# A hybrid attention and state-space layer on one core: another order of the seven block products, the second token half's index queries before the first's, the first conv group in pairs, and a third pair of buffers for split weights

## The chip, the core and the metric

The kernel runs on one core of a Trainium2 chip. The metric is the time of one execution on the device in microseconds (us); less is better. Each time is the median of several runs on one chip, and one more execution was taken by the hardware profiler. In the profile, PE is the matrix engine, PEld its loading of the stationary operand, DVE the vector engine, ACT the scalar (activation) engine, POOL the general engine, and SP the engine whose queue issues the DMAs.

## The reference, cut to what matters

One layer over 1024 tokens of width 2048. All input projections are one product with `w_in`; its columns are then split by use.

```
u = einsum('bsd,de->bse', h, w_in)
q, k, v, z_attn, q_idx, k_idx, w_idx, z_ssd, xbc, dt_raw = split(u)
# indexer: 16 heads of 64, keys in chunks of 64; the top 256 keys of each query
logits = relu(einsum('bqhd,bsd->bqhs', rope(q_idx), rope(k_idx)))
score  = einsum('bqhs,bqh->bqs', logits, w_idx * c), causal by chunk
o_attn = attention(q, k, v over the selected keys) * silu(z_attn)
# mixer: causal depthwise conv (4 taps) and silu on xbc, then a scan over chunks
o_ssd  = gated_rmsnorm(ssd(silu(conv(xbc)), dt), silu(z_ssd))
h = layer_norm(alpha * h + concat(o_attn, o_ssd) @ w_out)
```

Everything is float32. The conv needs the last three tokens of the first half as its start in the second half.

## The kernel before, in words

**Precision.** A float32 operand is split on chip into a rounded high part and a remainder (`hi` on ACT, `lo = x - hi` on DVE, or on POOL where the planner's method `two`, line 473, picks it). A product of two such operands is three matmuls, hi·hi, hi·lo and lo·hi (lines 1181 to 1183 for the input projection). Weights are split in `w_split` (line 916) from a raw tile `wr` into `wh` and `wl`, 128x1024 each, that is a block of 1024 rows of the depth by 128 columns. Tokens are split in `t_xst` (line 766) into `xh` and `xl`, 128x512 each.

**Input projection.** Tokens stand in two halves (h = 0 the first 512, h = 1 the rest), the depth in two halves (u = 0 and 1). A *set* is one token half by one depth half, or a sum of such blocks: eight pairs `xh`, `xl`. There are 16 slots of each, so two sets are on chip at a time, and a set's slots come free one by one in the last product that reads it. A *product* is one set by one weight block into one PSUM tile `pj`: 8 pieces of the depth by 3 matmuls, 24 matmuls. A *plain* column tile takes two products for each token half, so eight in all for two tiles and both halves. A *pair* of column tiles is done with a Winograd scheme in seven products (`product`, line 665), over sets that are blocks of x or sums of them: `M2`, `M3`, `S1`, `S4` are made once by `t_xform` (line 783) and kept in device memory. A pair runs in four phases, with two products in each of the first three and one in the last. Between phases partial results (`P1`, `U2`, `U3`) go to device memory and back, and where a product needs a sum of weight blocks, `t_wacc` (line 880) makes it on DVE from raw tiles.

**Order of the work.** `PLAN` (line 56) lists the stages; a stage in round brackets is plain, one in square brackets is a group of pairs, in which phase by phase all pairs are passed. `misc` holds the indexer's keys and head weights and the mixer's dt; `qi` are the eight tiles of index queries (two heads each); `xbc` of group g is four tiles (two of x, one of B, one of C). For `qi` of the first half only the last 256 tokens are computed, as the first 256 have at most 256 keys to choose from: those products are 24 matmuls of 128x256 (`s0`, line 607).

```
PLAN = [
    (0, FIRST + [("xbc", (0, 2)), ("xbc", (0, 3))], 2),
    (1, [("misc", 0)] + QI + [("xbc", (0, j)) for j in range(4)], 3),
    [(("k", 0), ("k", 1)), (("v", 0), ("v", 1))] + [(("q", n), ("q", n + 4)) for n in range(4)],
    (0, QI, 3),
    [(("xbc", (1, j)), ("xbc", (3, j))) for j in range(4)] + ... # 14 pairs in all
]
```

So there are five stages: first half `misc` and conv group 0; second half `misc`, `qi` and conv group 0; the *first group*, six pairs of k, v and q; first half `qi`; the *second group*, 14 pairs. Then comes the output projection, seven products of 8 blocks (`PRODUCTS`, line 68), whose sums of `w_out` are made in the background by `t_wsum` (line 814) during the input projection.

**Index scores and selection.** When a `qi` tile is done, `t_qi` (line 1455) ropes and splits it and then adds, for each of its heads, each block of 128 queries and each half of the keys, two matmuls into a PSUM tile `a` and a task `t_score` (line 1496): a relu on ACT in place, and a multiply-add on DVE into the running score tile. The second half has 8 tiles x 2 heads x 4 blocks x 2 key halves = 128 such scores, the first half 32. When all are in, `t_topk` (line 1520) finds the threshold by 32 sweeps of ACT over the scores, each followed by three tiny DVE operations.

**What sets the order.** The program is written by a planner in Python: `Flow` (line 354) with a model of the engines `Sim` (line 132). It walks the products in their order on PE and between them emits background tasks when its model says that their inputs, buffers and engine are ready. On the chip each engine runs its own queue in the order written, with semaphores between. SP's queue holds nearly all DMAs, in order, so that a waiting DMA holds up those behind it.

Of the kernel before, what the change touches and what calls it, by code (L numbers as in the profile page):

```python
# [15 lines left out]
D = 2048  # L16
S = 1024
HALF = 512
P = 128
# [10 lines left out]
NU = 28  # L30
# [11 lines left out]
def tile_order():  # L42
# [10 lines left out]
FIRST = [("misc", 0), ("xbc", (0, 0)), ("xbc", (0, 1))]  # L53
KVQ = [("k", 0), ("k", 1), ("v", 0), ("v", 1)] + [("q", n) for n in range(8)]
# [77 lines left out]
class Sim:  # L132
# [154 lines left out]
    def dma(self, eng, out, in_, kw):  # L287
# [9 lines left out]
        self.clk["D"] = x + max(out.size(), in_.size()) * 4 * (1 / 400 + 0.6 / row)  # L297
# [259 lines left out]
class Piece:  # L557


    def __init__(self, kind, h=0, t=0, u=0, **kw):  # L560
        self.kind, self.h, self.t, self.u = kind, h, t, u
        self.load, self.keep, self.s0, self.n, self.last = (), (), 0, None, False
        self.open = self.close = True
        self.done = self.after = None
        self.hold = self.base = False
        self.op = ALU.add
        self.__dict__.update(kw)


class Layer:  # L570
    def __init__(self, ctx, tc, a):
# [7 lines left out]
        for tag, n in (("xh", 16), ("xl", 16), ("xr", 2), ("wr", 5), ("wh", 2), ("wl", 2), ("u", NU), ("s4", N4), ("cv", 2), ("sm", 6)):  # L579
            fl.add_tag(tag, pool("p_" + tag, bufs=1), n)  # L580
# [10 lines left out]
    def units(self):  # L591
# [3 lines left out]
        self.sets = []  # L595

# [15 lines left out]
        for pairs in PLAN:  # L612
# [10 lines left out]
            a11 = len(self.sets)  # L623
            base = a11 + 1
            self.sets += [("x", 1, 0), ("f", "M2"), ("f", "M3"), ("x", 0, 1), ("f", "S1"), ("f", "S4"), ("x", 1, 1)]
            n = [(a11, base), (base + 1, base + 2), (base + 3, base + 4)]
# [3 lines left out]
            for ph in range(3):  # L630
                for couple in couples:
                    for f in range(2):
                        for c in couple:
                            i = put(self.product(gi, c, pairs[c], ph, f, n[ph][f]))
                            if ph and not (ph == 1 and f == 1):
                                self.hooks.setdefault(max(i - 1, 0), []).append(lambda gi=gi, c=c, ph=ph, f=f: self.pre_ld(gi, c, ph, f))
            for c in range(len(pairs)):
                i = put(self.product(gi, c, pairs[c], 3, 0, base + 5))
                self.hooks.setdefault(i - 1, []).append(lambda gi=gi, c=c: self.pre_ld(gi, c, 3, 0))
# [25 lines left out]
    def product(self, gi, c, pair, ph, f, n):  # L665
# [7 lines left out]
        p = Piece("T", load=load, keep=keep, n=n, open=f == 0, close=True, skip=f == 1, key=(gi, c, ph),  # L673
                  hold=ph < 2 and f == 0, base=ph < 2 and f == 1)
        if f:
            p.after = self.ev_after(gi, c, ph)
        out = lambda h, k: (pair[k][0], h, pair[k][1])

        def done(ps):
            at = fl.t + 100  # L680
            if ph == 0:
                fl.add(self.t_save(gi, c, f, ps), 0, f"save{gi}{c}{f}", at)
            elif ph == 1 and f == 0:
                fl.add(self.t_u3(gi, c, ps), 0, f"u3{gi}{c}", at)
            else:
                kind, h, j = out(0, 0) if ph == 1 else out(0, 1) if ph == 2 and f == 0 else out(1, 1) if ph == 2 else out(1, 0)
                fl.add(self.t_comb(gi, c, ph, f, kind, h, j, ps), 0, f"{kind}{j}h{h}", at)
# [12 lines left out]
    def t_save(self, gi, c, f, ps):  # L700
# [4 lines left out]
        fl.act(x, ps)  # L705
        if f:
            fl.free(ps)
        else:
            fl.signal(self.ev_after(gi, c, 0))
        yield Need("")  # L710
        name = ("P1", "U2")[f]
# [4 lines left out]
    def t_u3(self, gi, c, ps):  # L716
        fl = self.fl
        yield Need("V", u=1, ev=(self.ev_ld[gi, c, 1, 0],))
        x = fl.new("u", [P, HALF])
        fl.tt("V", x, ps, self.ld[gi, c, 1, 0], ALU.add)  # L720
        fl.signal(self.ev_after(gi, c, 1))
        yield Need("")
        fl.dma(self.p_scr("U3", gi, c), x)
        fl.free(x)
        fl.signal(self.ev_save["U3", gi, c])

    def pre_ld(self, gi, c, ph, f):
        name = "P1" if ph == 3 else "U3" if (ph, f) == (2, 0) else "U2"
# [10 lines left out]
    def t_comb(self, gi, c, ph, f, kind, h, j, ps):  # L739

        fl = self.fl
        key = (gi, c, ph, 0 if ph == 1 else f)
        yield Need("V", ev=(self.ev_ld[key],), **({"cv": 1} if kind == "xbc" else {}))
        x = self.ld.pop(key)
        op = ALU.subtract if ph == 2 else ALU.add
        u = fl.new("cv", [P, 3 + HALF]) if kind == "xbc" else None
        fl.tt("V", x if u is None else u[:, 3:3 + HALF], ps, x, op)
        if (ph, f) == (2, 0):
# [3 lines left out]
        if u is None:  # L752
            yield from getattr(self, "s_" + kind)(h, j, x)
        else:
            yield from self.s_xbc(h, j, x, u)
# [27 lines left out]
    def t_xform(self, kp):  # L783
# [4 lines left out]
        for tag, h, u in (("s4", 0, 0), ("s4", 0, 1), ("xr", 1, 0)):  # L788
# [16 lines left out]
        fl.dma(d, self.a["xt"][1, 4 + kp])  # L805
# [8 lines left out]
    def t_wsum(self, half):  # L814
# [11 lines left out]
        for d in range(2):  # L826
            for j in range(4):
                yield Need("D", u=2, keep=6)
                x, y = load("B22", d, j), load("B12", d, j)
                yield Need("V")  # L830
                fl.two(x, x, y, ALU.subtract)
                yield Need("D", us=1)
                save("T3", d, j, x)
                fl.free(x)
# [3 lines left out]
                fl.free(z)  # L838
# [1449 lines left out]
```

## Time and profile before

| | us |
|---|---|
| median of 3 runs | 1727.53 |
| lowest and highest run | 1725.99, 1731.79 |
| the profiled execution's own time | 1725.14 |
| its span, first to last instruction | 1723.4 |

The profiled execution thus has 1.7 us around its span, and its time lies 2.4 us under the median. How to read the profile: a row of groups gives an instruction's line, engine, operation, what it writes and reads, shapes, how many, then its busy time and mean duration, then the idle time of the engine before it and what ended that. Nearly every instruction carries line 313, a helper, so tiles tell them apart: `pj` is PSUM for products, `a` PSUM for scores and transposes, `wr` a raw weight tile, `u` and `s4` general buffers (`s` in some rows). A table of windows gives busy time and count of each engine in a stretch of the span, then PEclk, the granted clock of PE as a share of full speed. Matmuls overlap: one of 128x512 is reported with some 390 ns, but the next may start 227 ns later, so a full PE shows as busy throughout, and work is counted by starts, not by busy time.

### The profile page before, as it was taken

What the parts mean: (1) busy time and instruction counts of PE and PEld (TensorE: products, weight loads), DVE (VectorE), ACT (ScalarE), POOL (GpSimd) and SP (SyncE); (2) the same over time, 40 slices, a digit from 0 to 9 for tenths busy, and PEclk for the clock granted to TensorE, in tenths of its full rate; (3) what the DMA queues carried; (4) which work ended last, traced back from release to release, by engine and by line L of the source; (5) the groups of instructions that cost most, each with busy time, mean ns of one, the idle gap of its engine ahead of it and who ended that gap; (6) DMA issues with size and microseconds to landing.
All of it is one profiled execution on the core that took longest, in us unless ns stands there. A gap on an engine that the chain in (4) does not pass through costs nothing. (4 is left out here: it accounts for less than half of the span.)

```text
span 1723.4 us, 24378 instructions
## 1 busy us (share of the span) xinstructions
PE 1638.7 (95%) x8044; PEld 1351.2 (78%) x8044; DVE 1353.0 (79%) x2444; ACT 1019.6 (59%) x1799; POOL 173.5 (10%) x201
## 2 busy tenths in 40 slices
PE   9999999998887989999999999989999999999997
PEld 7877788876666978778888788877888877888875
DVE  5779999787567898789996788845777677659998
ACT  5745575678666856987555478456867544532320
POOL 0000010000000000000222111222121110000110
PEclk9999999999899999999999999999999999999998
DMA  9576578988787678989666875658778999877654
GB/s 320 202 253 230 198 258 290 324 310 307 246 294 259 222 266 271 315 299 318 227 220 219 312 236 188 220 186 251 241 230 280 313 314 342 298 278 268 218 193 147
DMA packets 210215, 446.50 MB, mean 259 GB/s; under 512 B 21928, under 2 KB 61992, under 8 KB 210088
## 3 DMA queue, kind: packets, MB, share of 16 engines
q1 hardware_dynamic: 209656, 444.55, 75.9%
q8 instruction: 63, 1.03, 0.2%
q14 instruction: 64, 0.52, 0.1%
q10 hardware_dynamic: 432, 0.39, 0.1%
HBM read 338.56 MB, written 106.30 MB: 258 GB/s over the span
## 5 line engine op out<-in xcount | busy, mean ns | idle before, releaser
L313 PE MATMUL pj<-xh,wh 128*128 128x512 f32 (+1 forms) x1192 | 470.0, 394 | 25.9 <-ACT wh L313 18.0
L313 PE MATMUL pj<-xh,wl 128*128 128x512 f32 (+1 forms) x1192 | 460.1, 386 | 9.3 <-DVE wl L313 9.1
L313 PE MATMUL pj<-xl,wh 128*128 128x512 f32 (+1 forms) x1192 | 458.8, 385 | 0.1
L313 DVE TENSOR_TENSOR wl<-wr,wh 128x1024 fp32r<-128x1024 f32 (+1 forms) x179 | 213.9, 1197 | 113.2 <-ACT wh L313 112.6
L313 PEld LDWEIGHTS pj<-xh,wh 128*128 128x128 f32 x1192 | 227.1, 191 | 70.7 <-ACT wh L313 20.6
L313 PEld LDWEIGHTS pj<-xh,wl 128*128 128x128 f32 x1192 | 226.5, 190 | 58.8 <-DVE wl L313 14.4
L313 PEld LDWEIGHTS pj<-xl,wh 128*128 128x128 f32 x1192 | 227.3, 191 | 41.2 <-DVE xl L313 1.8
L313 ACT ACTIVATE wh<-wr 128x1024 fp32r<-128x1024 f32 (+1 forms) x185 | 190.6, 1033 | 106.7 <-PE pj L313 67.2
L313 PE MATMUL pj<-xh,s 128*128 128x512 f32 (+1 forms) x688 | 222.1, 385 | 1.8 <-DVE u L313 1.6
L313 PE MATMUL a<-u,u 128*128 128x512 f32 (+3 forms) x746 | 171.7, 351 | 16.4 <-DVE u L313 7.0
L313 PEld LDWEIGHTS a<-u,u 128*128 128x128 f32 x746 | 123.3, 189 | 50.1 <-DVE s L313 10.6
L313 PEld LDWEIGHTS pj<-xh,s 128*128 128x128 f32 x688 | 127.7, 188 | 27.3 <-ACT xh L313 2.3
L313 DVE TENSOR_TENSOR u<-u,u 128x512 f32<-128x512 f32 (+7 forms) x212 | 130.2, 627 | 16.1 <-DMA u<-wo 4.5
L313 ACT ACTIVATE u<-s,sm 128x768 bf16<-128x768 f32 (+7 forms) x132 | 129.6, 982 | 21.3 <-DVE sm L313 19.5
L313 DVE TENSOR_TENSOR wr<-wr,wr 128x1024 f32<-128x1024 f32 (+1 forms) x98 | 121.6, 1243 | 20.5 <-DMA wr<-wt 19.4
L313 ACT ACTIVATE u<-a 128x512 fp32r<-128x512 f32 (+4 forms) x115 | 53.4, 479 | 138.0 <-DVE u L313 66.5
L313 PE MATMUL pj<-xl,s 128*128 128x512 f32 (+1 forms) x344 | 130.8, 380 | 0.8 <-DVE xl L313 0.8
L313 ACT ACTIVATE u<-u 128x512 f32<-128x512 f32 (+4 forms) x165 | 91.9, 566 | 61.5 <-DVE u L313 57.3
L313 ACT ACTIVATE a<-a 128x512 f32<-128x512 f32 (+3 forms) x160 | 76.1, 504 | 70.3 <-PE a L313 69.2
L313 DVE TENSOR_TENSOR s<-wr,s 128x1024 fp32r<-128x1024 f32 (+2 forms) x59 | 70.8, 1200 | 30.7 <-ACT s L313 30.5
L313 DVE TENSOR_TENSOR u<-pj,u 128x512 f32<-128x512 f32 (+2 forms) x94 | 62.4, 664 | 36.7 <-PE pj L313 31.0
L313 PE MATMUL pj<-wh,xh 128*128 128x512 f32 x218 | 87.8, 403 | 1.2 <-DVE u L313 1.2
(253 smaller groups left out, 2678.9 us busy)
## 6 DMA issues: line engine op xcount, KB each, us to landing
wr<-wt SPq DMA_DIRECT2D x228, 512.0 KB, 5.3
u<-u SPq DMA_DIRECT2D x100, 256.0 KB, 5.7
u<-wo SPq DMA_DIRECT2D x79, 256.0 KB, 5.1
wr<-ts SPq DMA_DIRECT2D x32, 512.0 KB, 5.7
ts<-u SPq DMA_DIRECT2D x63, 256.0 KB, 4.3
xr<-xt SPq DMA_DIRECT2D x28, 512.0 KB, 4.9
s<-xt SPq DMA_DIRECT2D x28, 512.0 KB, 6.6
u<-mx SPq DMA_DIRECT2D x49, 256.0 KB, 6.3
```

What stands on the lines that cost most here:

```text
L313: f(*args, **kw)
```

## The change

The core of the diff; what is left out are the plumbing of the partial results' names, and the loops' unchanged lines.

```diff
-NU = 28
+NU = 29
...
-FIRST = [("misc", 0), ("xbc", (0, 0)), ("xbc", (0, 1))]
+FIRST = [("misc", 0), ("qi", 0), ("qi", 1)]
 PLAN = [
-    (0, FIRST + [("xbc", (0, 2)), ("xbc", (0, 3))], 2),
-    (1, [("misc", 0)] + QI + [("xbc", (0, j)) for j in range(4)], 3),
-    [(("k", 0), ("k", 1)), (("v", 0), ("v", 1))] + [(("q", n), ("q", n + 4)) for n in range(4)],
-    (0, QI, 3),
+    (1, FIRST + QI[2:], 3),
+    (0, [("misc", 0)] + QI, 3),
+    [(("k", 0), ("k", 1)), (("v", 0), ("v", 1))] + [(("q", n), ("q", n + 4)) for n in range(4)]
+    + [(("xbc", (0, 2 * j)), ("xbc", (0, 2 * j + 1))) for j in range(2)],
...
-        self.clk["D"] = x + max(out.size(), in_.size()) * 4 * (1 / 400 + 0.6 / row)
+        self.clk["D"] = x + max(out.size(), in_.size()) * 4 * (1 / 360 + 0.6 / row)
...
-        for tag, n in (("xh", 16), ("xl", 16), ("xr", 2), ("wr", 5), ("wh", 2), ("wl", 2), ("u", NU), ("s4", N4), ("cv", 2), ("sm", 6)):
+        for tag, n in (("xh", 16), ("xl", 16), ("xr", 2), ("wr", 6), ("wh", 3), ("wl", 3), ("u", NU), ("s4", N4), ("cv", 2), ("sm", 6)):
...
-            self.sets += [("x", 1, 0), ("f", "M2"), ("f", "M3"), ("x", 0, 1), ("f", "S1"), ("f", "S4"), ("x", 1, 1)]
+            if self.sets[-2:] != [("x", 0, 0), ("x", 0, 1)]:
+                self.sets += [("x", 0, 0), ("x", 0, 1)]
+            base = len(self.sets) - 2
+            self.sets += [("f", "M2"), ("f", "M3"), ("f", "S1"), ("f", "S4"), ("x", 1, 1)]
...
-        t3 = ("s", "T3", gi, c)
-        load, keep = [[((b11,), ()), ((b22, b12), (t3,))], [((t3,), ()), ((b11, b21), ())],
-                      [((b12, b11), ()), ((b22,), ())], [((b21,), ())]][ph][f]
+        t2 = ("s", "T2", gi, c)
+        load = [[(b11,), (b21,)], [(b22, b12, b11), ()], [(t2, b22), ()], [(t2, b21)]][ph][f]
...
-        for tag, h, u in (("s4", 0, 0), ("s4", 0, 1), ("xr", 1, 0)):
+        for tag, h, u in (("s4", 1, 0), ("s4", 1, 1), ("xr", 0, 0)):
...
-        for hh, st in ((0, a1), (1, a2)):
-            head = 2 * j + hh
...
-                for kh in range(h + 1):
...
+        for kh in range(h, -1, -1):
+            for hh, st in ((0, a1), (1, a2)):
+                head = 2 * j + hh
...
+        if first:
+            yield Need("A", cv=1, ev=(self.ev_carry[4 * j[0] + j[1]],))
+            u = fl.new("cv", [P, 3 + HALF])
+            fl.act(u[:, 3:3 + HALF], x)
...
-    nc = bacc.Bacc("TRN2", target_bir_lowering=False, num_devices=1)
+    nc = bacc.Bacc("TRN2", target_bir_lowering=False, num_devices=1, dynamic_dma_scratch_size=1024)
```

In words. **Stages.** There are four input stages in place of five: second half `misc` and `qi`; first half `misc` and `qi`; the first group, now eight pairs with conv group 0 as two of them; the second group as before, 14 pairs. Conv group 0 has no plain products any more. **Products of a pair.** Still seven in four phases, but the first phase is first token half by `b11` and by `b21`, the next `M2` and `M3`, then `S1` and `S4`, then the second half's second depth block. The weight block of a phase's second product is what is left of the first's sum (the new table `mate`): one list of loads in the second and the third phase serves two products. A pair loads 9 raw tiles in place of 10, and DVE makes 4 sums of them in place of 5. **Sets.** The first half's two sets are those that the stage ahead of the first group has used, and they stay. **Scores and conv.** In `t_qi` the scores of a tile go by key half, the queries' own half first. In `t_comb` a conv tile's second-half result can come ahead of its first-half result, and then waits in a buffer for the carried tokens. **Buffers.** A sixth raw tile, a third `wh` and `wl`, one more `u`; the scratch for the DMA rings of the general engine is set to 1024 bytes. **Output weights.** `t_wsum` keeps a tile that it used to load twice.

The planner writes the queues anew. Two places.

The first is PE's queue in the `qi` stage of the first token half. Before, these rows stand near the stage's start (`pj` is the product, `xh` and `xl` the tokens, `wh` and `wl` the weights):

```order
L313 MATMUL pj_5256<-xh_4845,wh_5123 128x256
L313 MATMUL pj_5256<-xl_4846,wh_5123 128x256
L313 MATMUL pj_5256<-xh_4845,wl_5124 128x256
L313 MATMUL pj_5256<-xh_4849,wh_5123 128x256
L313 MATMUL pj_5256<-xl_4850,wh_5123 128x256
L313 MATMUL pj_5256<-xh_4849,wl_5124 128x256
```

Now, in the same stage (`a` is a score's PSUM tile, `u_1716` to `u_1718` the first half's keys, `u_687` and `u_797` queries of the second half):

```order
L312 MATMUL pj_2076<-xl_1369,wh_1936 128x256
L312 MATMUL pj_2076<-xh_1368,wl_1937 128x256
L312 MATMUL a_2121<-u_1716,u_687 128x512
L312 MATMUL a_2121<-u_1718,u_687 128x512
L312 MATMUL a_2124<-u_1716,u_797 128x512
L312 MATMUL a_2124<-u_1717,u_797 128x512
L312 MATMUL a_2127<-u_1716,u_687 128x512
L312 MATMUL a_2127<-u_1718,u_687 128x512
L312 MATMUL pj_2076<-xh_1416,wh_1993 128x256
```

The narrow products stood by themselves; now the second half's scores against the first half's keys stand between them.

The second is SP's queue where the first group goes to its second phase: the sets (`xfM` is `M3` before and `M2` now, `xt` a block of x) and weights (`wt`). Before, from the middle of the loads of the first of the two sets:

```order
L313 DMA s_605_3316<-xfM_107 128x1024
L313 DMA s_610_3326<-xfM_108 128x1024
L313 DMA xr_3336<-xt 128x1024
L313 DMA p_0_5_3344<-u_3328 128x512
L313 DMA xr_3346<-xt 128x1024
L313 DMA wr_3359<-wt 128x1024
L313 DMA wr_3360<-wt 128x1024
L313 DMA s_620_3369<-xt 128x1024
L313 DMA s_625_3396<-xt 128x1024
```

Now, from the start of the loads of the first set:

```order
L312 DMA xr_3483<-xfM_109 128x1024
L312 DMA xr_3485<-xfM_110 128x1024
L312 DMA s_609_3487<-xfM_111 128x1024
L312 DMA s_610_3489<-xfM_112 128x1024
L312 DMA q_0_293<-u_3466 4x32x512
L312 DMA wr_3527<-wt 128x1024
L312 DMA wr_3528<-wt 128x1024
L312 DMA wr_3529<-wt 128x1024
L312 DMA t_0_0_3540<-wr_3425 128x1024
```

The four loads of a set stand in one run, ahead of the phase's weight loads, where they were spread among other transfers and those of the second set; three raw tiles are loaded at once for the two products of a pair, and their sum of two is kept (`t_0_0`).

More of the change, by code (lines that the diff above doesn't have):

```diff
@@ L705, in t_save, with t_u @@
         fl.act(x, ps)
+        fl.signal(self.ev_after(gi, c, 0))
+        yield Need("")
+        fl.dma(self.p_scr("P1", gi, c), x)
+        fl.free(x)
+        fl.signal(self.ev_save["P1", gi, c])
+    def t_u(self, gi, c, f, ps):
+        fl = self.fl
+        name = ("U2", "U3")[f]
+        yield Need("V", ev=(self.ev_ld[gi, c, 1, 0],), **({} if f else {"u": 1}))
+        y = self.ld[gi, c, 1, 0]
+        x = y if f else fl.new("u", [P, HALF])
+        fl.tt("V", x, ps, y, ALU.add)
         if f:
@@ L714, in t_save @@
         fl.signal(self.ev_save[name, gi, c])
[L716 to L725, printed above, removed]
     def pre_ld(self, gi, c, ph, f):
-        name = "P1" if ph == 3 else "U3" if (ph, f) == (2, 0) else "U2"
+        name = "P1" if ph == 1 else "U2" if f else "U3"
         e = self.ev_ld[gi, c, ph, f] = Event()
@@ L741, in t_comb @@
         fl = self.fl
-        key = (gi, c, ph, 0 if ph == 1 else f)
-        yield Need("V", ev=(self.ev_ld[key],), **({"cv": 1} if kind == "xbc" else {}))
+        key = (gi, c, ph, f)
+        first = (ph, f) == (2, 0)
+        cv = kind == "xbc" and not first
+        yield Need("V", ev=(self.ev_ld[key],), **({"cv": 1} if cv else {}))
         x = self.ld.pop(key)
[L745 to L748, printed above, removed]
+        u = fl.new("cv", [P, 3 + HALF]) if cv else None
+        fl.tt("V", u[:, 3:3 + HALF] if cv else x, ps, x, ALU.subtract if ph == 2 else ALU.add)
+        if first:
             fl.signal(self.ev_after(gi, c, 2))
@@ L751, in t_comb @@
             fl.free(ps)
[L752 removed]
+        if kind != "xbc":
             yield from getattr(self, "s_" + kind)(h, j, x)
[L754 to L755 removed]
+            return
+        if first:
+            yield Need("A", cv=1, ev=(self.ev_carry[4 * j[0] + j[1]],))
+            u = fl.new("cv", [P, 3 + HALF])
+            fl.act(u[:, 3:3 + HALF], x)
+        yield from self.s_xbc(h, j, x, u)
     def form_tasks(self):
@@ L863, in w_load @@
         fl = self.fl
+        if not p.load:
+            return
         if len(p.load) > 1:
@@ L956, in need_w @@
                 self.nld += 1
-            fl.drain(until=lambda: k not in self.wacc and self.w_room(), why="w")
+            fl.drain(until=lambda: k in self.wraw and self.w_room(), why="w")
             self.w_split(k)
@@ L1513, in t_score @@
                 fl.free(*self.kk[1])
-            else:
+            if sum(self.nlog) == 160:
                 fl.free(*self.kk[0])
@@ L1666, in s_v, with t_zs @@
         fl.signal(self.ev_kv[h, g, "v"])
+    def t_zs(self, h, gj, ps):
+        fl = self.fl
+        yield Need("A", u=1)
+        x = fl.new("u", [P, HALF])
+        yield from self.s_zs(h, gj, x, ps)
     def s_z(self, h, n, x):
```

156 lines of the change are left out of this document (73 added, 83 removed).

## The prediction

> **What bounds the kernel now.** The page's busy list comes first.
>
> ```profile
> PE 1638.7 (95%) x8044; PEld 1351.2 (78%) x8044; DVE 1353.0 (79%) x2444; ACT 1019.6 (59%) x1799; POOL 173.5 (10%) x201
> ```
>
> PE is the bound, so the time is PE's work plus what PE loses, and the work has to be counted. The timeline of PE gives the price of a matmul from start to start where nothing waits: eleven starts of the 128x512 form, then six of the 128x256 form.
>
> ```profile
> 701.05 0.39 PE L313 MATMUL pj<-xh,wl 128*128 128x512 f32 x1
> ...
> 703.32 0.39 PE L313 MATMUL pj<-xh,wh 128*128 128x512 f32 x1
> ```
>
> ```profile
> 548.77 0.28 PE L313 MATMUL pj<-xh,wh 128*128 128x256 f32 x1
> ...
> 549.37 0.28 PE L313 MATMUL pj<-xh,wl 128*128 128x256 f32 x1
> ```
>
> That is (703.32 - 701.05) / 10 = 0.227 us and (549.37 - 548.77) / 5 = 0.12 us. A product of 24 is 5.45 us, a narrow one 2.9. Next come windows cut at the stages: phases two to four of the first group, the narrow stage (first half `qi`), the second group in two pieces.
>
> ```profile
> core 0: us, PE busy (x) PEld busy (x) DVE busy (x) ACT busy (x) POOL busy (x), PEclk, DMA share, GB/s
> 340.00:548.00 208.00, 183.40 (x795) 144.96 (x795) 149.70 (x316) 145.63 (x267) 4.88 (x3) 0.96 0.84 290
> 548.00:615.00 67.00, 52.77 (x409) 50.81 (x409) 57.45 (x116) 52.46 (x87) 2.81 (x2) 0.92 0.67 237
> 680.00:1100.00 420.00, 415.44 (x2106) 347.03 (x2105) 343.94 (x679) 287.93 (x521) 63.24 (x64) 1.00 0.77 259
> 1100.00:1200.00 100.00, 91.24 (x472) 75.06 (x471) 57.53 (x117) 51.80 (x85) 19.82 (x19) 0.98 0.69 219
> ```
>
> The second group's first 420 us leave PE idle for 4.6 us. The first group's 208 leave 24.6, and the clock there is 0.96, another 0.04 x 208 = 8.3: 33 together. The count of work says the same. PE's groups by shape in 340:548:
>
> ```profile
> L313 PE MATMUL pj<-xh,wh 128*128 128x512 f32 x190 | 78.6, 413 | 15.1 <-ACT wh L313 7.3 <-ACT xh L313 6.8 <-DVE sm L313 0.8
> L313 PE MATMUL pj<-xh,wl 128*128 128x512 f32 x191 | 77.5, 406 | 5.0 <-DVE wl L313 5.0
> L313 PE MATMUL pj<-xl,wh 128*128 128x512 f32 x190 | 76.6, 403 | 0.1
> L313 PE MATMUL pj<-xh,s 128*128 128x512 f32 x96 | 31.4, 394 | 1.6 <-DVE u L313 1.6
> L313 PE MATMUL pj<-xl,s 128*128 128x512 f32 x48 | 18.7, 390 | 0.0
> ```
>
> These 715 take 162.3 us, the other 80 are at most 256 wide in this answer, so at most 9.6: 172 of 208, a loss of 36. The narrow stage in the same way:
>
> ```profile
> L313 PE MATMUL pj<-xh,wh 128*128 128x256 f32 x91 | 26.9, 296 | 9.1 <-ACT wh L313 9.1
> L313 PE MATMUL pj<-xh,wl 128*128 128x256 f32 x91 | 26.9, 295 | 2.0 <-DVE wl L313 2.0
> L313 PE MATMUL pj<-xl,wh 128*128 128x256 f32 x91 | 26.5, 292 | 0.0
> L313 PE MATMUL pj<-xh,s 128*128 128x256 f32 x64 | 12.9, 282 | 0.0
> L313 PE MATMUL pj<-xl,s 128*128 128x256 f32 x32 | 9.0, 282 | 0.0
> ```
>
> 369 x 0.12 = 44.3, the other 40 at most 0.227 each and mostly narrower, an estimated 6: some 51 of 67, a loss of 16. Each narrow product asks for a weight block of 512 KB every 2.9 us, 180 GB/s for weights alone, and its split by ACT and DVE besides.
>
> The waits of PE tell what the first group's idle time is made of (total, times, longest):
>
> ```profile
> PE pj L313 <- ACT wh L313: 7.3, 2, 5.8
> PE pj L313 <- ACT xh L313: 6.8, 2, 3.5
> PE pj L313 <- DVE wl L313: 5.0, 4, 3.6
> ```
>
> They are few and long: a split weight block or set that comes late when the sets are switched, with a DMA share of 0.84 and much of ACT's time taken.
>
> **The change, part by part.** All sums are made against the profiled execution, 1725.14 us; it lies 2.4 below the median of 1727.53, and I add that at the end.
>
> *Conv group 0 in pairs.* Four tiles took 16 plain products; two pairs take 14. 2 x 24 = 48 matmuls of 128x512 go, 48 x 0.227 = **-10.9 us**. In the order of the two programs nothing else differs on PE in number (5920 against 5872 of this shape). This is on the bound itself; the bounds are 0 and -10.9, since time saved on PE can turn into waiting.
>
> *The first group's waits.* Phases two to four make five switches of sets in both versions, but over 8 pairs x 5 = 40 products in place of 30, so 8 products (44 us) stand between switches in place of 6 (33 us). At each switch SP has four set loads of 512 KB in front of the weights (the second place of the order shown above): 2.1 MB at the window's 290 GB/s is 7.2 us. A split pair in reserve is one product, 5.45 us; the third `wh` and `wl` give a second, 10.9 us of cover against 7.2, and the sixth raw tile one more loaded behind it. The waits for `wh` and `wl`, 7.3 + 5.0 = 12.3, should go, and with the long idle stretches gone the clock's 8.3. The waits for `xh`, 6.8, are not covered by a weight buffer; with 8 products in place of 6 I take off a third, 2.3. Together **-23**, of a loss of 36; bounds 0 (what is late is the set, and the weights only stood behind it) and -36. Next late is then `xh`.
>
> *The narrow stage.* First half `qi` now stands right behind the second half's `qi`, and second-half scores lie between its narrow products, as the order shows. Scores need PE and no weights: between PE's rows 440 and 1342 of the new order, the latter at the end of the narrow products, I count 264 product matmuls of 128x512, 384 of 128x256, 176 score matmuls of 128x512 and 85 smaller, 158 us of PE work for about 27 weight blocks, one per 5.8 us in place of 2.9. The weight wait goes: **-16**. Bounds 0 and -16; if half stays, +8 on the sum.
>
> *What the scores ask of DVE there.* The nearest stretch of before is that of second-half scores, 126.5 to 222.8.
>
> ```profile
> 126.50:222.80 96.30, 94.31 (x424) 75.61 (x423) 91.86 (x140) 58.22 (x108) 4.22 (x3) 1.00 0.57 202
> ```
>
> DVE is busy 95% of it. PE's groups there, by shape:
>
> ```profile
> L313 PE MATMUL pj<-xh,wh 128*128 128x512 f32 x97 | 38.3, 395 | 0.0
> L313 PE MATMUL pj<-xh,wl 128*128 128x512 f32 x96 | 37.5, 390 | 0.0
> L313 PE MATMUL pj<-xl,wh 128*128 128x512 f32 x96 | 37.4, 390 | 0.0
> L313 PE MATMUL a<-u,u 128*128 128x512 f32 x83 | 24.5, 402 | 1.7 <-DVE s L313 1.6
> ```
>
> 372 x 0.227 = 84.4, and 52 smaller at some 0.13: 91 of 96.3, a loss of 5. For the new stretch I price DVE's 292 rows with the groups of the whole trace:
>
> ```profile
> L313 DVE TENSOR_TENSOR wl<-wr,wh 128x1024 fp32r<-128x1024 f32 x173 | 210.9, 1221 | 108.0 <-ACT wh L313 107.3
> L313 DVE TENSOR_TENSOR u<-u,u 128x512 f32<-128x512 f32 x133 | 90.1, 687 | 10.7 <-DMA u<-wo 4.5 <-DMA u<-rq 2.4 <-DMA u<-mx 2.0
> L313 DVE SCALAR_TENSOR_TENSOR s<-a,wsc,s 128x512 f32<-128x512 f32 x75 | 54.4, 745 | 4.2 <-ACT a L313 3.5
> L313 DVE SCALAR_TENSOR_TENSOR s<-a,wsc,s 128x384 f32<-128x384 f32 x15 | 9.2, 610 | 0.9 <-ACT a L313 0.8
> ```
>
> 41 x 1.22 + 82 x 0.745 + 22 x 0.61 + 36 x 0.687 + 111 smaller at an estimated 0.43 (under the least of these, 0.61) = 197 us for 158 of PE. Not all of it must be done there: of the 159 rows that the order of before has beside the PE rows of its stretch, the trace has 140 done in the time, 88%. 0.88 x 197 = 173, a loss of 15 in place of 5: **+10**. Bounds: -5 (DVE keeps up) and 197 - 158 - 5 = +34 (nothing can be put off).
>
> *The scans of group 0* end up in the second group. Cost between 0 (680:1100, where PE idles for 1% only) and the 8.8 us that PE idles in 1100:1200, the group's worst stretch; I take **+3**, nearer the first.
>
> *Costed at nothing.* One sum of raw tiles and one raw load less per pair, the sets that stay (four set loads and splits fewer for each group), `t_wsum`'s saved loads: DVE, ACT and SP work under PE's, and their gain is in the waits above. The eight copies on ACT for conv tiles whose halves come in the other order, priced by
>
> ```profile
> L313 ACT ACTIVATE u<-u 128x512 f32<-128x512 f32 (+4 forms) x165 | 91.9, 566 | 61.5 <-DVE u L313 57.3
> ```
>
> are 8 x 0.57 = 4.5 us on an engine that is 59% busy; behind the wait for the carried tokens stand ACT's splits of weights, which three pairs now cover. Without that cover 4.5 is the price. The entry to the second group switches two sets before and after. The scratch for the general engine's rings: no such queue does work in the trace, 0.
>
> Sum: -10.9 - 23 - 16 + 10 + 3 = **-36.9**; 1725.1 - 36.9 = 1688.2, and + 2.4 = **1691 us**.
>
> **The rivals.** *All switches hidden.* If DMA, being asked for less (9 raw tiles a pair in place of 10), also brings sets in time, the first group's whole 36 goes: 13 less, 1678. For it: the second group, with the same five switches over 14 pairs, idles only 4.6 in 420 us. Against: that is 14 products a switch, not 8, and no top-k on ACT beside it.
>
> *The first group's waits stay.* If what is late is the set, behind ACT's top-k sweeps (ACT is 70% busy in 340:548), a third weight buffer only moves the wait: +23, 1714; with half of the narrow stage's loss also staying, 1722. For it: the waits for `xh`, and top-k of the second half still falls in this group, joined by the first half's.
>
> *The score stage runs at a halved clock: slower.* In the new stretch PE alternates between short products and scores through three PSUM tiles, and has to wait for DVE at many of them. After idle time the clock falls:
>
> ```profile
> 160.00:200.00 40.00, 39.62 (x181) 32.37 (x180) 38.30 (x59) 24.62 (x50) 0.00 (x0) 1.00 0.51 183
> ...
> 508.00:512.00 4.00, 3.32 (x7) 2.22 (x8) 3.05 (x5) 1.42 (x4) 0.00 (x0) 0.50 0.99 360
> ```
>
> The second row follows the wait of 5.8 us for `wh`; PEclk is 0.50. If waits for `a` do this to half of the stretch's 158 us of work, that half takes twice as long, +79 in place of +10: 1760. The other terms give -46.9, so it decides when over 47 of the 158, 30%, run at half clock. Against: in 160:200 scores cycle through the same three tiles with DVE 96% busy, and the clock is 1.00.
> By the Trainium skill, page TensorE: Matmul & The Clock Gate, section "A second HAM failure mode: psum-queue depth-cycling", short idle times between groups of matmuls that cycle through PSUM banks make the clock go to and fro between half and full, which would be this rival; 160:200 does not bear that out for idle times this short, and only the longer wait before 508:512 does something like it.
>
> **How the numbers follow.** The forecast 0.50; all hidden 0.15; first group's waits stay 0.25; halved clock 0.10. A difference under 0.3%, 5 us, can't be told from no change by a measurement of this kernel. Of the third case a sixth (0.04) and of the fourth 0.03 (a milder form, near the 30%) end within it, so same is 0.07, slower 0.07, faster 0.86. The range goes down to 1665: all hidden, less the +10 and the +3; and up to 1720, just short of the third case with half of the narrow loss. It leaves out most of the halved clock, the top of the third case, and the DVE bound of +34 on top of that case: under 0.2.
>
> **What the profile after would show.** Right: 5872 matmuls of 128x512 in count; waits of PE for `wh` and `wl` in the first group well under 12 us with those for `xh` the longest left, and PEclk 0.99 or more there; narrow products with gaps under 1 us and scores between; DVE over 90% busy and PE idle 10 to 20 us in the score stretch. Wrong: a single wait over 5 us for `wh` in phases two to four (the third buffer does not cover a switch); PEclk under 0.9 in the score stretch (the halved clock); DVE busy through and PE idle 30 us there; or a new wait at the start of the first group, which I cost at nothing.

## The result, and the profile after

The changed kernel takes 1707.31 us in the median of 4 runs (1706.45 to 1709.86), the kernel before on the same chip 1728.64 (4 runs). The ratio is 0.988 with a 95% interval of 0.9861 to 0.9899: 1.2% faster, some 21 us. The forecast was 1691, 36 us faster, with a range of 1665 to 1720.

The page of the changed kernel gives PE 48 matmuls less, and still as the bound:

```profile
PE 1631.9 (96%) x7996; PEld 1347.0 (79%) x7996; DVE 1328.9 (78%) x2411; ACT 985.3 (58%) x1750; POOL 174.2 (10%) x198
```

To see where the other 10 us went, I cut both kernels at their stages. First the kernel before: start and second-half scores, first group, narrow stage, second group, output projection.

```profile
0.00:258.90 258.90, 250.72 (x1110) 200.65 (x1111) 211.77 (x328) 154.82 (x263) 15.91 (x33) 0.99 0.69 244
258.90:546.60 287.70, 262.83 (x1157) 210.18 (x1156) 218.90 (x428) 193.68 (x349) 11.69 (x13) 0.97 0.85 295
546.60:615.70 69.10, 54.87 (x425) 52.89 (x424) 59.36 (x119) 52.46 (x87) 2.81 (x2) 0.93 0.68 239
615.70:1359.40 743.70, 725.59 (x3689) 604.03 (x3688) 574.52 (x1121) 489.11 (x888) 111.38 (x129) 1.00 0.76 253
1359.40:1723.40 364.00, 344.64 (x1669) 283.49 (x1667) 288.47 (x451) 129.55 (x212) 31.73 (x24) 0.98 0.77 258
```

Then the changed kernel: start, narrow stage with the scores, first group, second group, output projection. The columns are again PE, PEld, DVE, ACT, POOL, PEclk, DMA share and GB/s.

```profile
0.00:131.50 131.50, 127.43 (x575) 101.73 (x576) 100.56 (x171) 71.03 (x130) 7.58 (x17) 1.00 0.67 234
131.50:254.30 122.80, 104.03 (x575) 84.33 (x574) 114.56 (x181) 69.03 (x118) 6.52 (x5) 0.90 0.52 185
254.30:597.40 343.10, 329.42 (x1438) 269.08 (x1437) 284.33 (x616) 272.50 (x526) 17.88 (x26) 0.99 0.79 281
597.40:1329.40 732.00, 726.32 (x3789) 609.33 (x3788) 547.41 (x1008) 446.27 (x779) 115.90 (x132) 1.00 0.75 252
1329.40:1704.40 375.00, 344.71 (x1626) 282.56 (x1625) 282.06 (x438) 126.47 (x199) 26.32 (x19) 0.96 0.73 246
```

Busy time hides a slow clock, so from here on *loss* is a stage's length less its recorded matmuls at their price from start to start at full clock (0.2265, 0.175, 0.120 and 0.109 us for 512, 384, 256 and 128 columns, 0.217 for bf16). It sums to the difference of the spans, 1723.4 - 1704.4 = 19.0:

| | before | after | change | forecast |
|---|---|---|---|---|
| matmuls (1588.2 and 1577.4 us) | | | -10.9 | -10.9 |
| loss in the first group | 38.6 | 22.3 | -16.3 | -23 |
| loss in start, scores and narrow stage | 18.2 + 17.3 | 9.2 + 36.7 | +10.4 | -16 + 10 |
| loss in the second group | 36.1 | 18.4 | -17.7 | +3 |
| loss in the output projection | 24.9 | 40.3 | +15.4 | 0 |

The first group's waits of PE, the rows that answer to those of before (`wh` 7.3, `xh` 6.8, `wl` 5.0):

```profile
PE pj L312 <- DVE u L312: 4.5, 1, 4.5
PE pj L312 <- ACT u L312: 3.4, 1, 3.4
...
PE pj L312 <- ACT wh L312: 1.8, 1, 1.8
PE pj L312 <- DVE sm L312: 1.1, 1, 1.1
PE pj L312 <- DVE wl L312: 0.5, 1, 0.5
```

Of the 12.3 us for `wh` and `wl` 2.3 are left, and none for `xh`. What is late now is a PSUM tile that DVE or ACT has still to read out (the waits on `u`). The same kind stands in the narrow stage. PE's longest wait there, and DVE's queue ahead of it:

```profile
134.51 0.75 DVE L312 SCALAR_TENSOR_TENSOR s<-a,wsc,s 128x512 f32<-128x512 f32 x1
135.18 1.22 DVE L312 TENSOR_TENSOR s<-s,s 128x1024 f32<-128x1024 f32 x1
136.43 1.23 DVE L312 TENSOR_TENSOR s<-xr,s 128x1024 f32<-128x1024 f32 x1
137.57 1.22 DVE L312 TENSOR_TENSOR wl<-wr,wh 128x1024 fp32r<-128x1024 f32 x1
138.71 1.41 DVE L312 TENSOR_TENSOR u<-u,u 128x512 f32<-128x512 f32 x2
...
142.05 0.69 DVE L312 TENSOR_TENSOR u<-pj,u 128x512 f32<-128x512 f32 x1
```

```profile
142.88 0.55 PE L312 MATMUL pj<-xh,wh 128*128 128x256 f32 x1 [7.59 <-DVE u L312]
143.24 0.41 PE L312 MATMUL pj<-xl,wh 128*128 128x256 f32 x1
143.45 0.41 PE L312 MATMUL pj<-xh,wl 128*128 128x256 f32 x1
```

There are four `pj` tiles, and the next is still held by a finished product. It is free when DVE has roped it (the last step is `u<-pj,u`), and ahead of that in DVE's queue stand two sums of token blocks (`s<-s,s`, `s<-xr,s`: `t_xform`), a weight split and two sums of `w_out` (`u<-u,u`: `t_wsum`). These five take 4.9 us and are only the last of the rows ahead. Counted by 24 matmuls, the product had been done at 118.9: from there to the start of its read-out at 140.05, DVE's queue holds 21 us of rows.

```profile
118.94:140.05 21.11, 16.35 (x89) 14.03 (x87) 20.84 (x32) 11.54 (x20) 0.00 (x0) 0.94 0.84 303
```

At that point two of the four tiles hold finished products of the second half, the other two products of the new stage of which the first depth half is done. After the wait the starts lie 0.21 us apart in place of 0.12. The clock in that place:

```profile
135.00:139.00 4.00, 0.29 (x3) 0.09 (x1) 3.97 (x5) 1.06 (x1) 0.00 (x0) 0.83 0.54 186
139.00:143.00 4.00, 0.12 (x1) 0.15 (x1) 3.86 (x8) 0.23 (x1) 0.00 (x0) 0.50 0.98 331
143.00:147.00 4.00, 4.00 (x19) 4.00 (x20) 3.90 (x7) 1.03 (x2) 0.00 (x0) 0.50 1.00 354
147.00:151.00 4.00, 4.00 (x21) 3.52 (x20) 3.85 (x7) 2.23 (x4) 1.04 (x2) 0.89 0.92 280
```

One wait of 7.6 us thus costs some 10. Over the narrow stage PE is idle for 122.8 - 104.0 = 18.8 us. The clock's shortfall is 0.10 x 122.8 = 12.3 us, that is some 24 us at half clock, but in 7.4 of these PE is idle anyway (as in the first two windows above). So the clock takes another 8 us, together 27 of the loss of 36.7; the other 10 are not taken apart.

The second longest wait, 4.4 us, has POOL in it:

```profile
203.34 2.34 POOL L312 TENSOR_TENSOR s<-s,s 128x1024 f32<-128x1024 f32 x1 [53.57 <-DMA xr<-xt]
203.43 0.43 DVE L312 TENSOR_TENSOR pj<-pj,u 128x256 f32<-128x256 f32 x1
203.76 2.20 DVE L312 TENSOR_TENSOR u<-u,u 128x256 f32<-128x256 f32 x1
205.99 0.42 DVE L312 TENSOR_TENSOR u<-pj,u 128x256 f32<-128x256 f32 x1
...
206.56 0.55 PE L312 MATMUL pj<-xh,wh 128*128 128x256 f32 x1 [4.39 <-DVE u L312]
```

Here the planner put a sum of token blocks on POOL. The third step of the read-out takes 2.20 us beside it, and 0.41 in the next read-out (at 220.08): 1.8 of the 4.4 us. All four `pj` tiles hold finished products then: five `qi` products of the stage were done by 197.2, and one had been read out.

### The profile page after: what moved, and what is told of

Read it like the earlier page. It is cut to its first block, busy times and chain, and to the rows that moved or that the text cites. A ratio compares the mean times of both kernels' runs of the same rounds, so it can differ in the third digit from the quotient of the medians.

```text
span 1704.4 us, 24034 instructions
## 1 busy us (share of the span) xinstructions
PE 1631.9 (96%) x7996; PEld 1347.0 (79%) x7996; DVE 1328.9 (78%) x2411; ACT 985.3 (58%) x1750; POOL 174.2 (10%) x198
## 4 chain that ended last, share of the span: by engine, by line
PE 53%; DVE 19%; ACT 11%; DMA 10%; issue 5%; SPq 1%; POOL 1%; DVEq 0%; ACTq 0%
PE pj L312 39%; PE a L312 11%; DVE u L312 8%; ACT u L312 5%; DVE wl L312 3%; DVE s L312 3%; PE o L312 3%; ACT wh L312 2%; DVE wr L312 2%; DMA wr<-wt 2%; DVE xl L312 1%; SPq L312 1%; DMA s<-xt 1%; DMA u<-xt 1%; DMA u<-o 1%
## 5 line engine op out<-in xcount | busy, mean ns | idle before, releaser
L312 PE MATMUL pj<-xh,wh 128*128 128x512 f32 (+1 forms) x1496 | 587.8, 393 | 27.1 <-DVE u L312 20.1
L312 PE MATMUL pj<-xl,wh 128*128 128x512 f32 (+1 forms) x1496 | 574.0, 384 | 1.2 <-DVE xl L312 1.1
L312 PE MATMUL pj<-xh,wl 128*128 128x512 f32 (+1 forms) x1496 | 574.0, 384 | 0.5 <-DVE wl L312 0.5
L312 DVE TENSOR_TENSOR wl<-wr,wh 128x1024 fp32r<-128x1024 f32 (+2 forms) x232 | 278.0, 1202 | 183.8 <-ACT wh L312 176.9
L312 ACT ACTIVATE wh<-wr 128x1024 fp32r<-128x1024 f32 (+2 forms) x242 | 248.4, 1031 | 189.8 <-PE pj L312 153.6
L312 DVE TENSOR_TENSOR u<-u,u 128x512 f32<-128x512 f32 (+6 forms) x231 | 149.7, 660 | 10.5 <-DMA u<-o 4.2
L312 ACT ACTIVATE u<-s,sm 128x768 bf16<-128x768 int16 (+7 forms) x132 | 129.5, 981 | 1.5
L312 PE MATMUL pj<-wh,xl 128*128 128x512 f32 x310 | 122.3, 395 | 2.3 <-DVE xl L312 2.3
L312 PE MATMUL pj<-wl,xh 128*128 128x512 f32 x310 | 122.3, 394 | 0.0
L312 POOL TENSOR_SCALAR s<-s,sm 128x640 f32<-128x640 f32 (+7 forms) x64 | 60.1, 953 | 245.9 <-DVE sm L312 188.6
```

Source lines behind the costliest of these rows:

```text
L312: f(*args, **kw)
```

## The experiments

Three questions: what makes the narrow stage lose 36.7; what took the first group's waits away; and how much of the result is owed to the order that the planner happened to write. My theory for the first, **D**: DVE has more to do in the stage than PE, by its 197 us of priced rows against 158, and the stretch of those rows (PE's rows 440 to 1342 of the order, 99.8 to 298.4 us in the trace) did take 198.6. (It runs on for 44 us behind the last narrow product, which starts its last matmul at 254.2.) Rival **C**: not the sum of DVE's work but a few products' read-out behind background rows, and the clock after that. Twelve kernels were run, each for three rounds or more beside the kernel before; the ratios are to that, and the changed kernel has 0.988.

### The third pair of split weights

```diff
-("wr", 6), ("wh", 3), ("wl", 3)
+("wr", 5), ("wh", 2), ("wl", 2)
```

> The changed kernel with five raw tiles and two pairs wh, wl, as before. If the third pair of split weights is what took the first group's waits away (19 us less loss there than before), most of it comes back: 12 to 19 us slower than 1707, with waits for wh and wl at the switches of sets. If it was the rarer switches and the set loads in one run, within 4 us of 1707 and no such waits.

Measured: 1756.32 us, ratio 1.0183 (1.0149 to 1.0217), 49 us slower than the changed kernel, far outside what either theory said. Waits of PE in its first group, with those for weights back (2.3 us before the edit, 18.0 now):

```profile
PE pj L312 <- ACT wh L312: 11.2, 5, 4.2
PE pj L312 <- DVE wl L312: 6.8, 7, 2.2
```

The first group's loss is 38.1 in place of 22.3; that is the 16 us expected. The second group loses 50.0 in place of 18.4 and the output projection 53.8 in place of 40.3, and PE's largest sum of waits in the second group is for read-outs by DVE:

```profile
PE pj L312 <- DVE u L312: 19.0, 6, 8.4
```

The edit takes the third pair and the sixth raw tile away together. So the new order of products does need these buffers, and the rest of the 49 has another source.

The same buffers in the kernel before, with its own order:

```diff
-("wr", 5), ("wh", 2), ("wl", 2)
+("wr", 6), ("wh", 3), ("wl", 3)
...
-num_devices=1)
+num_devices=1, dynamic_dma_scratch_size=1024)
```

> The kernel before with the changed kernel's six raw tiles, three pairs of split weights and the ring scratch of 1024 bytes; all else as before. If the buffers alone took the first group's waits away: 15 to 25 us faster than before, ratio 0.986 to 0.991, the first group's loss from 42 to some 20. If they only serve the new order of the products, within 6 us of before.

Measured: 1717.71, ratio 0.9942 (0.9925 to 0.9958), 10 us faster. The first group's loss falls from 38.6 to 21.3, as if by the whole change, so buffers alone take those waits away, again the third pair and the sixth raw tile together. Of the 17 us, some are given back at once: at the switch to the second group, 604 to 621 us, PE stands still for 15 of 17.

```profile
604.00:621.00 17.00, 2.23 (x7) 1.15 (x6) 16.83 (x32) 7.41 (x14) 0.00 (x0) 0.63 0.33 123
```

DVE is busy throughout that window: a new wait behind DVE.

### DVE's load in the narrow stage

```diff
-            fl.stt(sc, r[:, 0:m], wcol, sc, ALU.mult, ALU.add)
+            if not (h == 1 and kh == 0 and head % 2):
+                fl.stt(sc, r[:, 0:m], wcol, sc, ALU.mult, ALU.add)
```

> The changed kernel without the multiply-add of every second head's scores against the first half's keys: 32 DVE operations of 0.745 us, 23.8 us, are left out, and their share of the scores is missing. Theory D (the score stage takes as long as DVE's work in it, 197 us by price and 198.6 measured): 18 to 24 us faster, 1683 to 1689, the stage near 176 us. Rival C (a few waits for a product's PSUM tile behind background work in DVE's queue, and the halved clock after them, whatever the sum of DVE's work): at most 6 us faster.

Measured: 1714.84, ratio 0.9944 (0.9927 to 0.9961): slower than the changed kernel, which fits neither. By stage it does: the narrow stage's loss is 21.4 in place of 36.7, but the first group loses 39.4 in place of 22.3 and the second 29.1 in place of 18.4. The first group's waits for split weights are back, with all the buffers in place:

```profile
PE pj L312 <- ACT wh L312: 7.1, 3, 3.9
PE pj L312 <- DVE wl L312: 5.7, 4, 2.5
```

The planner counts on the 32 rows being gone and writes another order for all that follows. An edit that it sees can't be judged by the total. So the next one hides the edit from it: `ghost` lets the planner's model run and emits nothing.

```diff
+            if not self.flow.ghost:
+                f(*args, **kw)
...
+            fl.ghost = h == 1 and kh == 0 and head % 2 == 1
             fl.stt(sc, r[:, 0:m], wcol, sc, ALU.mult, ALU.add)
+            fl.ghost = False
```

> As a2_half_scores, the 32 multiply-adds are left out (their share of the scores is missing), but the planner still counts them, so that every engine's queue is the changed kernel's with 32 rows less on DVE. Theory D: the score stage 15 to 24 us shorter and, as nothing else is planned anew, the whole 12 to 24 us faster than the changed kernel, ratio to before 0.974 to 0.981. Rival C: at most 6 us, 0.985 or more.

Measured: 1697.84, ratio 0.9828 (0.9812 to 0.9845), 9 us faster: between the two. The second of the pair takes the sums of token blocks away in the same manner, by `fl.ghost` around each `fl.two` of `t_xform`.

> As b1_same_order_half, and the 16 sums of token blocks are left out too (the sets that need them hold plain blocks, so most outputs are wrong in value), in the changed kernel's order: 32 x 0.745 + 15 x 1.22 = 42 us less on DVE, most of it in the score stage. Theory D (DVE's work beyond PE's is the loss): the narrow stage's loss falls from 36.6 over 23.7 in b1 to 10 or less, as DVE then has less to do there than PE; 25 to 32 us faster than the changed kernel in all, ratio 0.969 to 0.974. If the rest of 23.7 is not DVE's work (the order of queues, weights), it stays near 20 and the ratio at 0.98 or more.

Measured: 1692.73, ratio 0.9804 (0.9774 to 0.9834). The narrow stage in the two, b1 first:

```profile
132.00:242.40 110.40, 95.92 (x577) 81.64 (x576) 95.97 (x156) 67.41 (x118) 6.55 (x5) 0.95 0.59 208
```

```profile
132.00:238.50 106.50, 93.59 (x572) 81.81 (x571) 82.80 (x143) 66.45 (x118) 4.18 (x4) 0.95 0.61 212
```

DVE's busy time falls from 114.6 over 96.0 to 82.8, from 93% of the stage to 87% and 78%. The loss goes from 36.7 to 23.7 and then only to 20.7. The first 18.6 us off DVE's busy time bring 13.0, the next 13.2 bring 3.0. That is as if DVE's load were the bound, as D has it, until it falls under some 90% of the stage. But much of the 13.0 comes by the way that C names: PE's waits for read-outs fall from 15.6 to 12.3 us, in b1 the collision with POOL does not hit the read-out, and PE works some 7 us at half clock in place of 16.5, which is 5 us. So the two runs show that the loss hangs on these rows, and do not part their sum from their place in the queue. The long wait is still there in c1 with two 1.22 us rows less ahead of it, only 1.2 us shorter, since DVE then waits 1.09 us for a `wh`:

```profile
141.77 0.55 PE L313 MATMUL pj<-xh,wh 128*128 128x256 f32 x1 [6.39 <-DVE u L313]
```

So 16 of the 36.7 us hang on the DVE rows left out, and D falls as the whole account. That 198.6 us passed for 197 us of priced rows was partly chance: DVE was busy for 184.86 of them.

Background out of the stage, in ways that the planner sees. First `t_wsum` alone, later:

```diff
-            self.hooks.setdefault(12, []).append(lambda half=half: ... "wsum"))
+            self.hooks.setdefault(36, []).append(lambda half=half: ... "wsum"))
```

> The changed kernel with t_wsum alone started with the first group in place of the twelfth product. Theory D: the 8 rows of 0.69 us that go from the stage, 5 us faster, 1701 to 1704. Rival C (the 7.6 us wait and the halved clock behind it hang on the background rows ahead of the product's eviction): 10 us or more faster.

Measured: 1716.22, ratio 0.9951 (0.9936 to 0.9966), slower by 9. Up to 300 us the loss is 38.6 in place of 48.8, a gain of 10 as C said; later places take 20 back, so it says little on its own.

The same, and the sums of token blocks on POOL (the first of four in `t_xform`; the others likewise):

```diff
-        yield Need("V")
-        fl.two(b, a, b, ALU.subtract)
+        yield Need("G")
+        fl.tt("G", b, a, b, ALU.subtract)
...
```

> The changed kernel with the 16 sums of token blocks (t_xform) forced to POOL and t_wsum started with the first group. Of DVE's rows between 131 and 254 us 11 of 1.22 us and 8 of 0.69 go, 19 us. Theory D: 12 to 19 us faster, 1688 to 1695, if POOL's operations leave DVE alone; if they hold DVE up, no gain or up to 10 us slower, with longer DVE operations beside them. Rival C: about the same gain, but with the two waits of over 4 us gone and DVE still below 95% busy.

Measured: 1729.42, ratio 1.002 (1.0006 to 1.0034), 22 slower. The narrow stage's loss is 31.9, a gain of 5. In a4, with `t_wsum` late and the sums still on DVE, it is some 25 (130.6 to 241.3 us), so as far as two plans can be compared POOL took back more than it gave. POOL's operations hold DVE's up; the timeline of POOL and DVE in that stage:

```profile
145.80 2.40 POOL L312 TENSOR_TENSOR xr<-s,xr 128x1024 f32<-128x1024 f32 x1
146.98 2.29 DVE L312 TENSOR_TENSOR wl<-wr,wh 128x1024 fp32r<-128x1024 f32 x1 [0.48 <-ACT wh L312]
```

The same DVE row takes 1.22 us by itself (137.57 above). Here it is done 1.07 us after POOL's end at 148.20, as if it had waited for nearly all of that. The Trainium skill, page SBUF — State Buffer, section "SBUF: two separate sides", says that an operation of DVE with two inputs in SBUF and one of GpSimd (POOL here) that reads SBUF lock each other out for a whole instruction; this row agrees, and so does that of 2.20 us in the changed kernel, which ends 0.28 us after POOL's. In the stage's 121 us DVE's splits average 1368 ns in place of 1219.

The sums later, on DVE:

```diff
-        self.hooks.setdefault(12, []).append(self.form_tasks)
+        self.hooks.setdefault(32, []).append(self.form_tasks)
```

> The changed kernel with the sums of token blocks started at the 33rd product, four products ahead of the first group, in place of the 13th: some 13 us of DVE leave the score stage for the first group, where DVE has room. Theory D: the loss up to the first group falls by 8 to 13, the whole gains that less what the new order does elsewhere (10 either way by theory N): ratio 0.977 to 0.990. If M2 then comes late, a wait at the second phase of the first group, up to 20 us, and slower than the changed kernel.

Measured: 1760.32, ratio 1.0196 (1.0168 to 1.0225). The narrow stage loses 19.5, 17 less; then the set `M2` is late at the first group's second phase:

```profile
366.77 0.80 PE L312 MATMUL pj<-xh,wh 128*128 128x512 f32 x1 [21.13 <-ACT xh L312]
407.53 0.79 PE L312 MATMUL pj<-xh,wh 128*128 128x512 f32 x1 [37.54 <-ACT xh L312]
```

This is the second outcome of the expectation, three times its size: the background that crowds the score stage is the sums that the next stage needs.

More PE work in the stage in place of less on DVE: conv group 0 plain again, between the index queries of both halves, first half first.

```diff
-FIRST = [("misc", 0), ("qi", 0), ("qi", 1)]
+FIRST = [("misc", 0), ("xbc", (0, 0)), ("xbc", (0, 1))]
+XBC = [("xbc", (0, j)) for j in range(4)]
-    (1, FIRST + QI[2:], 3),
-    (0, [("misc", 0)] + QI, 3),
+    (0, FIRST + [QI[0], XBC[2], QI[1], XBC[3]] + QI[2:], 3),
+    (1, [("misc", 0)] + [x for j in range(4) for x in (QI[j], XBC[j])] + QI[4:], 3),
...
-    + [(("xbc", (0, 2 * j)), ("xbc", (0, 2 * j + 1))) for j in range(2)],
...
-            self.x_load(1, k)
+            self.x_load(0, k)
```

> The changed kernel with conv group 0 as 16 plain products again, spread between the index queries of both halves, first half first; the first group has six pairs. 10.9 us more work on PE, and 87 us of PE work (with some 38 us on DVE) now beside the scores. Theory D: the loss up to the first group falls from 46 to 15 or 25, so 10 to 20 us faster than the changed kernel less plan effects of 10: ratio 0.978 to 0.990. If the loss is not DVE's excess over PE's work there: 10 us or more slower, 0.994 and up.

Measured: 1717.23, ratio 0.9948 (0.9931 to 0.9965), 10 slower. Up to the first group the loss is 18.8 in place of 45.9, a gain of 27 for 10.9 of work, as D has it. It is lost again in the second group (31.9 for 18.4) and in the output projection (52.4 for 40.3).

### The order of the stages

```diff
-FIRST = [("misc", 0), ("qi", 0), ("qi", 1)]
+FIRST = [("misc", 0), ("xbc", (0, 0)), ("xbc", (0, 1))]
 PLAN = [
-    (1, FIRST + QI[2:], 3),
-    (0, [("misc", 0)] + QI, 3),
+    (0, FIRST + [("xbc", (0, 2)), ("xbc", (0, 3))], 2),
+    (1, [("misc", 0)] + QI + [("xbc", (0, j)) for j in range(4)], 3),
...
-    + [(("xbc", (0, 2 * j)), ("xbc", (0, 2 * j + 1))) for j in range(2)],
+    (0, QI, 3),
...
-            self.x_load(1, k)
+            self.x_load(0, k)
```

> The changed kernel with the five stages of before (first half misc and conv group 0 plain, second half, first group of six pairs, first half qi alone, second group), with the new products, buffers and t_wsum. 48 matmuls come back, 10.9 us, and the two x sets of the first half are loaded two times more. My account: 10.9 more, the narrow stage alone loses 10 to 17 again, the score stage 20 to 25 less: within 6 us of the changed kernel, ratio 0.985 to 0.993. If the new order of the stages is what paid: ratio 0.995 or more.

Measured: 1707.98, ratio 0.9886 (0.9867 to 0.9904), the time of the changed kernel. With 10.9 us more work on PE it loses 9 us less: 23.0 at the start, 20.2 in the first group, 8.0 in the narrow stage by itself (17.3 before), 26.0 and 40.6 after. As these two plans came out, the new order of the stages with the pairs of conv group 0 thus brought nothing in sum: the 48 matmuls saved were paid back, in the score stage above all. The next runs show how far a single plan can be trusted.

### How much is the planner's order

The planner's model has a rate for DMA, which the change itself moved from 400 to 360. Two more values:

```diff
-        self.clk["D"] = x + max(out.size(), in_.size()) * 4 * (1 / 360 + 0.6 / row)
+        self.clk["D"] = x + max(out.size(), in_.size()) * 4 * (1 / 370 + 0.6 / row)
```

> The changed kernel with the planner's DMA rate at 370 in place of 360, the size of a neutral change: same work, another order. Theory N (the stalls at the switches of sets hang on the order that the planner happens to write, worth 10 us or more either way): off the changed kernel by 5 to 20 us, with the loss in other places. Theory S (the gain of the first group is settled by buffers and rarer switches): within 4 us of it.

> The changed kernel with the planner's DMA rate at 350, a second neutral change. Theory N: again another time than the changed kernel by 5 us or more either way. Theory S: within 4 us, and then the 9 us of b3_dma370 are worth a reason of their own.

Measured: at 370 1699.18, ratio 0.984 (0.9815 to 0.9865), 8 us faster; at 350 1723.23, ratio 0.9984 (0.9968 to 0.9999), 16 slower. The work is the same to the matmul, and the time ranges over 24 us, more than the change's 21. The losses by stage (start, narrow, first group, second group, output):

| rate | start | narrow | first group | second group | output | us |
|---|---|---|---|---|---|---|
| 350 | 10.5 | 29.7 | 28.8 | 30.0 | 47.4 | 1723.23 |
| 360, the change | 9.2 | 36.7 | 22.3 | 18.4 | 40.3 | 1707.31 |
| 370 | 9.5 | 25.4 | 25.7 | 30.0 | 26.2 | 1699.18 |

Theory N holds. The first group's 22 to 29 stay below the 38.6 of before in these draws, as in b4 (21.3) and a5 (20.2), which have the third pair in another order of stages; a2 with its 39.4 shows that even this gain is not safe from the order. The group's waits for `wh` and `wl` sum to 12.3 us in the kernel before and 18.0 in a1; with the third pair they are 0 in b4, 1.4 in a5 and a6, 6.6 at either rate, and 12.8 in a2. The second group's 18.4 and the output's 40.3 do not repeat: between 18 and 30 and between 26 and 47 the order alone decides. The version at 370 is the fastest of those with all the work, faster than before beyond its interval; its interval just meets that of the changed kernel.

## Why the prediction was right in direction and too high in size

**Conv group 0, -10.9: right.** The count fell from 8044 to 7996 and the work from 1588.2 to 1577.4.

**First group, -23: right in mechanism, measured -16.3.** I took 12.3 off for `wh` and `wl`; 10.0 went. The added buffers are the cause, by a1 (the waits and 16 us come back) and b4 (17 us go with the buffers alone, in the old order). That it is the third pair and not the sixth raw tile is not shown, and in a2's order both together do not keep the waits away. That 8 products in place of 6 between the switches were part of it is not shown: b4 has six pairs and does as well. I said that `xh` would be late next. It was not; the read-out of products was (`u`, 4.5 and 3.4 us). The clock's term, 8.3, did not all go, since those waits of over 3 us lower it as well: PEclk is 0.99 over the group, but 0.85 in the window with the longer of the two.

```profile
530.00:550.00 20.00, 14.42 (x52) 11.15 (x51) 16.68 (x31) 12.85 (x23) 1.24 (x2) 0.85 0.95 334
```


**Narrow stage, -16: its mechanism right.** No wait for weights is left in it. Its size can't be told from that of the next term, as both fall in one stage.

**Scores on DVE, +10: the step that failed.** I held that 12% of DVE's rows could be put off, 0.88 x 197, and so kept the loss at 15 where the bound without that was 39. The stage and the start together lost 45.9 in place of 35.5, so the two terms came to +10.4 and not to -6. The runs show two things in place of the 12%. DVE's rows were not put off: the sums of token blocks are needed in the next stage (c4), the scores before the selection; 16 us hang on the rows left out (b1, c1). And it matters where the rows stand: PE has four tiles for products, and a read-out behind 21 us of DVE's rows stops it for 7.6 us. I had these tiles in no term. Whether the read-outs stand so late for DVE's load alone, or also because the planner holds them back for free `u` buffers, no run tells.

The stretch itself was misread as well: row 1342 of the order is not the end of the narrow products, which lies near row 1150, and the counts take in five products of the first group. In the stretch as it was priced, PE's 158 us of work took 198.6, a loss of 40: the bound of 39 without the 12%, and not 15. DVE worked 184.9 us in it, where I had taken 173.

```profile
99.80:298.40 198.60, 178.86 (x913) 145.10 (x912) 184.86 (x311) 120.88 (x217) 10.73 (x12) 0.94 0.55 194
```

**The halved clock, a rival at 0.10: true in part.** Not short idle times between scores did it but, in the changed kernel, the three waits of 3 us and more for a read-out. Two windows that hold them:

```profile
131.00:150.00 19.00, 11.41 (x65) 10.75 (x64) 18.51 (x28) 5.69 (x9) 1.04 (x2) 0.73 0.89 302
...
200.00:239.00 39.00, 30.38 (x136) 23.62 (x137) 34.74 (x55) 20.04 (x36) 5.48 (x3) 0.82 0.37 136
```

PEclk is 0.73 and 0.82 there; in the stage PE works 16.5 us at half clock, which is 8 us of work, where 47 were needed to decide.
By the Trainium skill, page TensorE: Matmul & The Clock Gate, section "What's actually happening", the clock falls to half after an idle window of some 3.4 us. The trace agrees in kind, but here less was enough. The clock fell at 137.67, by the second row below, 2.4 us after the last matmul's end at 135.29, and was whole again at 147.9, 5 us after the matmuls started:

```profile
137.00:137.50 0.50, 0.00 (x0) 0.00 (x0) 0.50 (x1) 0.00 (x0) 0.00 (x0) 1.00 0.58 229
137.50:138.00 0.50, 0.00 (x0) 0.00 (x0) 0.50 (x2) 0.00 (x0) 0.00 (x0) 0.67 1.01 393
```

In b1 a wait of 2.2 us, up to 201.37, was enough:

```profile
202.00:205.00 3.00, 3.00 (x10) 2.45 (x9) 1.28 (x2) 1.37 (x3) 1.65 (x1) 0.50 0.18 72
```

**The second group, +3, and the output projection, 0.** Measured -17.7 and +15.4, nearly even. The three rates put these at 58.7 (360), 56.2 (370) and 77.4 us (350), against 61.0 before, so that neither difference can be put down to the scans of group 0 or to another step of the change; I had no term for the order itself. Why the output projection loses 26 in one order and 47 in another is not settled: its waits in the changed kernel are for the token splits (8.2 us, 2 times) and a read-out (7.0, once).

The sum of the terms was 17.8 us off. The score stage is 16.4 of that (+10.4 for -6); the first group's 6.7 and the last two stages' -5.3 nearly cancel, which owes something to chance, as the rates of 350 and 370 show; the chance of 0.86 for faster had the planner's draw in no case, and 350 would have come within 0.3% of before.

## What to carry to other kernels

Where a planner writes the queues, make the same edit in two ways, seen and unseen by it, and compare stage by stage; two neutral draws of the planner give the size below which a total says little (here 8 us one way and 16 the other). Before filling a stage that waits for weights with other work, add up what that work asks of the next engine, background rows and all, and take nothing off for what may be put off unless its deadline is known. Where PE waits for a read-out, look at when that product was done and at all that stands in between in the other engine's queue: PE can go on only until its PSUM tiles are taken. No run here changed their number.

## What the runs showed of the hardware

A wait of 7.6 us in PE costs about 10, since the clock stays at half for 4.8 us after it (starts 0.21 us apart until 147.7). Waits of up to 1.0 us left it whole (150 to 204 us of the changed kernel, PEclk 1.00), and one of 2.2 us did not (b1). An operation of 128x1024 takes POOL 2.4 us and DVE 1.22, and a DVE split that meets one on POOL takes 2.29: with the sums on an engine that is 10% busy and `t_wsum` late, the stage gained 5 us where 19 us of rows were to leave DVE.
